# Row copies from HBM to HBM for 14 of 128 tiles in a rank scatter on Trainium2

## The chip, the cores and the metric

The kernel runs on one core of a Trainium2 chip. The metric is the device time of one execution in microseconds (us). The time before is the median of three runs.

## What is computed

Each of eight batches has 2048 rows of 2560 float32 values (10240 bytes a row) and one score for each row. A row is written to the place that its score has in the ascending order of its batch. No row value is changed, so apart from the ranks the whole work is moving 167.8 MB from one place in HBM to another.

```python
B, N, D = 8, 2048, 2560
order = np.argsort(scores, axis=1)
ranks = np.argsort(order, axis=1)
out = np.zeros_like(x)
out[b_idx, ranks, :] = x      # b_idx = np.arange(B)[:, None]
```

## The kernel before

A tile is 128 consecutive rows of one batch, 1.31 MB; there are 16 tiles in a batch and 128 in all. A tile is loaded from HBM into one of 16 SBUF buffers (`xb`, one row in each partition), and later scattered from there to HBM by an indirect DMA that takes a row number for each partition from `rank_i`.

**Ranks.** The scores come in by one small DMA. TensorE transposes them into columns (line 140), then for each batch copies each column across all partitions (`broadcast`, lines 156 to 169) so that every partition holds all 2048 scores of the batch in `s_all`. For a tile, VectorE counts how many scores of the batch are smaller than each of its 128 scores, and how many equal ones stand ahead of it (`count`, line 225, in two or three pieces), adds the pieces (lines 248 and 254) and casts the rank to an integer (line 265). VectorE goes through batches and tiles in order.

**The order by hand.** The whole body is one critical section in which every wait is written out: a `Line` object stands for an engine and counts its finished instructions on a semaphore. Three queues move the data:

- SP and ACT issue the loads in turn (`load`, lines 289 to 296; loop at lines 325 to 332): even tiles on SP, odd tiles on ACT. Load k waits until scatter k - 16 has landed, because it takes that scatter's buffer (`scatter_done`, line 298). ACT does nothing else.
- POOL issues the scatters in tile order (lines 355 to 363). Scatter k waits until load k has landed and until VectorE has written the rank of that tile.
- After the last load, SP waits for the last 16 scatters (lines 338 and 339).

**What is there and unused.** `DIRECT` (line 56) lists, for each batch, tiles that don't go through SBUF. In the kernel before it is empty, so `BULK` (line 61) has all 128 tiles and `ROWS` (line 62) none; `chunks` (line 323) is empty, and the loops at lines 329 and 333 do nothing. The code for such tiles is complete:

- `from_psum` (lines 179 to 199) and line 270: TensorE transposes the column of 128 ranks into one row in PSUM, and VectorE turns it into byte offsets in `rows_i`, on one partition. This is done one tile later, when the next tile's rank has been added up.
- `rows` (lines 304 to 320) takes one chunk, 16 rows of a tile: it waits for that tile's offsets, loads the 16 offsets into registers of SP or ACT, and issues 16 DMAs, each of which copies one row of 10240 bytes from `x` to `out` at the offset in a register.

```python
while n < len(chunks) * (k - NBUF + 6) // (NB - NBUF + 6 + 6):
    rows(*two[n % 2], *chunks[n])
    n += 1
load(two[k % 2][0], k)
```

This loop sets how the chunks stand among the loads: even chunks on SP, odd ones on ACT, in proportion to the number of loads issued.

Of the kernel before, what the change touches and what calls it, by code (L numbers as in the profile page):

```python
# [40 lines left out]
def kernel(  # L41
# [7 lines left out]
    B, N, D = x.shape  # L49
# [3 lines left out]
    T = N // P  # L53


    DIRECT = [()] * B

    SPLIT = ()
    LAST = 2
    ORDER = [list(range(T)) for b in range(B)]  # L60
    BULK = [(b, t) for b in range(B) for t in ORDER[b] if t not in DIRECT[b]]
    ROWS = [(b, t) for b in range(B) for t in DIRECT[b]]
    NB = len(BULK)
# [28 lines left out]
    with tc.tile_critical(no_gpsimd_drain=True):  # L92
# [86 lines left out]
        def from_psum():  # L179
            b, t, tick = pending  # L180
            dve.after(pe, tick)
            col = b * T + t
            if t in DIRECT[b]:
                t_rows[b, t] = dve.did(
# [16 lines left out]
        for b in range(B):  # L201
# [12 lines left out]
            for t in ORDER[b]:  # L214
# [43 lines left out]
                if pending is not None:  # L258
                    from_psum()
                    pending = None  # L260
                direct = t in DIRECT[b]
                if not direct:
# [131 lines left out]
```

## Time and profile before

| what | value |
|---|---|
| median of three runs (lowest, highest) | 798.27 us (798.03, 798.38) |
| profiled execution, its own time | 798.03 us |
| span of the profiled execution | 796.3 us |
| bytes moved by the DMA queues | 335.74 MB, mean 422 GB/s |
| VectorE busy | 422.3 us |
| TensorE busy | 29.3 us |
| POOL busy (issuing 128 scatters, 949 ns each) | 122.6 us |
| last load issued, last scatter issued | 738.9 us, 749.2 us |

Times within the execution count from the span's start. "Busy" counts the work of an engine; waiting and the issue of DMAs by SP and ACT are not in it. The profile cuts the span into 40 equal slices of 19.9 us, and gives for each slice the busy share of each engine in tenths (9 is 90% or more), the busy share of the 16 DMA engines, and the bytes that they moved. A byte that is loaded and then scattered is counted twice there, once for each transfer. A DMA's time "to landing" runs from its issue to its semaphore.

### The profile page before, as it was taken

To read this page: it belongs to the slowest core of one execution; us is meant where nothing else is said; L and a number is where in the kernel's file an instruction comes from. 1 tells how busy PE (TensorE), PEld (TensorE's weight loads), DVE (VectorE), ACT (ScalarE), POOL (GpSimd) and SP (SyncE) were. 2 spreads that over 40 slices of the span, in tenths; PEclk is the share of its full clock that TensorE was granted. 3 is DMA by queue.
4 is the path that set the end of the run, shared out by engine and by line. 5 is a ranking of instruction groups with operands and counts; after the bars stand their busy time and mean duration, and the time that the engine had idled before them with its cause. 6 is when DMAs were issued, how large, how long until landed. Compare 5 with 4: busy or idle time off the path is not lost.

```text
span 796.3 us, 1925 instructions
## 1 busy us (share of the span) xinstructions
PE 29.3 (4%) x144; PEld 26.4 (3%) x144; DVE 422.3 (53%) x1170; POOL 122.6 (15%) x136
## 2 busy tenths in 40 slices
PE   3001001010010010010000000000000000000000
PEld 3001001010010010010000000000000000000000
DVE  6999999999999999999999200000000000000000
POOL 1211121111111111111111111111111111111100
PEclk9555555555555555555555555555555555555555
DMA  9999999999999999999999999999999999999995
GB/s 360 423 429 427 428 429 429 428 429 427 429 427 429 428 430 429 430 428 428 428 428 428 430 430 430 428 429 429 428 428 430 430 430 429 428 429 428 428 430 219
DMA packets 36893, 335.74 MB, mean 422 GB/s; under 512 B 4104, under 2 KB 4104, under 8 KB 4104
## 3 DMA queue, kind: packets, MB, share of 16 engines
q0 software_dynamic: 18432, 167.78, 49.7%
q10 hardware_dynamic: 9216, 83.89, 24.9%
q1 hardware_dynamic: 9232, 83.96, 24.9%
q14 instruction: 12, 0.10, 0.0%
q8 instruction: 1, 0.02, 0.0%
HBM read 167.84 MB, written 167.77 MB: 421 GB/s over the span
## 4 chain that ended last, share of the span: by engine, by line
another core or an unknown queue 81%; DMA 7%; DVE 3%; ACTq 2%; PE 1%; issue 0%; POOL 0%; SPq 0%; POOLq 0%
DMA out_dram<-x,rank_i 6%; ACTq L294 2%; DVE trash L225 2%; DMA x<-in_x_dram 1%; PE ps_all L161 0%; DMA s_in<-in_scores_dram 0%; PE ps_col L140 0%; DVE rank L254 0%; DVE rank L248 0%; POOL out_dram L345 0%; DVE rank_i L265 0%; DVE s_all L206 0%; DVE s_col L148 0%; SPq L389 0%
## 5 line engine op out<-in xcount | busy, mean ns | idle before, releaser
L225 DVE TENSOR_SCALAR_CACHE_REDUCE trash<-s_all,s_col 128x256 bf16<-128x256 f32 (+15 forms) x248 | 315.1, 1307 | 0.3
L345 POOL DMA_INDIRECT out_dram<-x,rank_i x128 | 121.5, 949 | 626.7 <-DMA x<-in_x_dram 435.6
L225 DVE SCALAR_TENSOR_TENSOR trash<-s_all,s_col,mask 128x128 bf16<-128x128 f32 x128 | 44.5, 347 | 0.0
L161 PE MATMUL ps_all<-ident,s_col 128*128 128x128 f32 x128 | 27.4, 403 | 307.8 <-DVE s_all L206 307.4
L161 PEld LDWEIGHTS ps_all<-ident,s_col 128*128 128x128 f32 x128 | 24.6, 215 | 310.3 <-DVE s_all L206 309.8
L254 DVE TENSOR_TENSOR rank<-rank,acc 128x1 f32<-128x1 f32 x128 | 20.5, 160 | 4.4
L248 DVE TENSOR_TENSOR rank<-acc,acc 128x1 f32<-128x1 f32 x128 | 20.4, 159 | 4.4
L265 DVE CAST rank_i<-rank 128x1 int32<-128x1 f32 x128 | 19.7, 154 | 4.5
L206 DVE COPY s_all<-ps_all 128x512 f32<-128x512 f32 x32 | 20.2, 684 | 2.2 <-PE ps_all L161 1.6
L225 DVE DVE_READ_ACCUMULATOR trash<-s_all,s_col 128x1 f32 x248 | 20.5, 83 | 0.0
L225 DVE DVE_READ_ACCUMULATOR trash<-s_all,s_col,mask 128x1 f32 x128 | 10.5, 82 | 0.0
L148 DVE COPY s_col<-ps_col 128x128 f32<-128x128 f32 x1 | 0.3, 292 | 4.6 <-PE ps_col L140 4.6
L140 PE MATMUL ps_col<-ident,s_in 8*128 8x8 f32 x16 | 1.9, 250 | 4.0 <-DMA s_in<-in_scores_dram 4.0
L140 PEld LDWEIGHTS ps_col<-ident,s_in 8*128 8x128 f32 x16 | 1.8, 216 | 4.0 <-DMA s_in<-in_scores_dram 4.0
L135 DVE MEMSET acc<- 128x128 f32 x1 | 0.2, 165 | 1.1 <-SPq L92 1.1
L111 POOL TENSOR_SCALAR_AFFINE_SELECT ident<-ident 128x128 f32<-128x128 f32 x1 | 0.3, 283 | 0.1
L123 POOL TENSOR_SCALAR_AFFINE_SELECT mask<-mask 128x128 f32<-128x128 f32 x1 | 0.3, 283 | 0.0
L107 POOL MEMSET ident<- 128x128 f32 x1 | 0.2, 204 | 0.5 <-SPq L92 0.5
L108 POOL MEMSET mask<- 128x128 f32 x1 | 0.2, 202 | 0.0
L378 POOL MEMSET const-float32-0.0<- 128x1 f32 x1 | 0.1, 99 | 0.3 <-issue 0.3
L378 POOL MEMSET const-uint8-127<- 128x1 uint8 x1 | 0.1, 120 | 0.0
L378 POOL MEMSET const-bfloat16-1.0<- 128x1 bf16 x1 | 0.1, 114 | 0.0
(1 smaller groups left out, 0.1 us busy)
## 6 DMA issues: line engine op xcount, KB each, us to landing
x<-in_x_dram ACTq DMA_DIRECT2D x64, 1280.0 KB
x<-in_x_dram SPq DMA_DIRECT2D x64, 1280.0 KB, 10.3
out_dram<-x,rank_i POOLq DMA_INDIRECT x128, 87.4
s_in<-in_scores_dram SPq DMA_DIRECT2D x1, 64.0 KB
```

The source lines that it names most:

```text
L111: nc.gpsimd.affine_select(out=ident[:], in_=ident[:], pattern=[[-1, P]], compare_op=OP.not_equal, fill=1.0, base=0, channel_multiplier=1,)
L123: nc.gpsimd.affine_select(out=mask[:], in_=mask[:], pattern=[[-1, P]], compare_op=OP.is_ge, fill=0.0, base=-1, channel_multiplier=1,)
L140: nc.tensor.transpose(out=ps_col[:, B * c:B * (c + 1)], in_=s_in[:, P * c:P * (c + 1)], identity=ident[:B, :B],)
L161: nc.tensor.transpose(out=ps_all[:, P * c:P * (c + 1)], in_=s_col[:, c, b:b + 1].to_broadcast([P, P]), identity=ident[:],)
L206: nc.vector.tensor_copy(out=s_all[:, 512 * q:512 * (q + 1)], in_=ps_all[:, 512 * q:512 * (q + 1)],)
L225: how.pop("do")(out=trash[i][:, :P * (hi_t - lo_t)], in0=s_all[:, P * lo_t:P * hi_t], accum_out=acc[which][:, cols], **how,)
L248: nc.vector.tensor_tensor(out=rank[:, cols], in0=acc[0][:, cols], in1=acc[1][:, cols], op=OP.add)
L254: nc.vector.tensor_tensor(out=rank[:, cols], in0=rank[:, cols], in1=acc[2][:, cols], op=OP.add)
L265: nc.vector.tensor_copy(out=rank_i[:, cols], in_=rank[:, cols])
L294: line.eng.dma_start(out=xb[i][:], in_=x[b, P * t:P * (t + 1), :]).then_inc(s_load[i], 16)
L345: nc.gpsimd.indirect_dma_start(out=out_flat, out_offset=bass.IndirectOffsetOnAxis(ap=index[:hi - lo, col:col + 1], axis=0), in_=xb[k % NBU ...
L378: nc = _bacc.Bacc("TRN2", target_bir_lowering=False, num_devices=1)
```

## The change

Two tiles (numbers 4 and 5) in each of the first six batches and one (number 4) in each of the last two are put on the list `DIRECT`; the rest of the code stays.

```diff
@@ -53,7 +53,7 @@
     T = N // P
 
 
-    DIRECT = [()] * B
+    DIRECT = [(4, 5)] * 6 + [(4,)] * 2
 
     SPLIT = ()
     LAST = 2
```

By it, 14 tiles (1792 rows) leave the load and scatter path. `BULK` has 114 tiles, so SP and ACT issue 57 loads each and POOL issues 114 scatters. `chunks` has 112 entries, 56 on each of SP and ACT, each with 16 register loads and 16 row copies; six of them stand ahead of load 16, eight behind the last load. For the 14 tiles TensorE does one more transpose and VectorE does the offset instruction at line 185 in place of the cast at line 265. Before the end, SP and ACT wait for all of their row copies (line 337).

## The prediction

> **What bounds the kernel now.** I read the slices first.
>
> ```profile
> DVE  6999999999999999999999200000000000000000
> POOL 1211121111111111111111111111111111111100
> DMA  9999999999999999999999999999999999999995
> GB/s 360 423 429 427 428 429 429 428 429 427 429 427 429 428 430 429 430 428 428 428 428 428 430 430 430 428 429 429 428 428 430 430 430 429 428 429 428 428 430 219
> ```
>
> The DMA row is full from the first slice to the middle of the last, at 427 to 430 GB/s in almost all of them. VectorE stops after slice 23 and the rate doesn't change: the ranks don't bound it. So the 16 DMA engines do. Then the queues:
>
> ```profile
> q0 software_dynamic: 18432, 167.78, 49.7%
> q10 hardware_dynamic: 9216, 83.89, 24.9%
> q1 hardware_dynamic: 9232, 83.96, 24.9%
> ...
> HBM read 167.84 MB, written 167.77 MB: 421 GB/s over the span
> ```
>
> Scatters (q0) take half of the engines' time, the loads of ACT (q10) and SP (q1) a quarter each, 99.5% together. Each DMA has 144 packets: 128 rows and one semaphore packet on each of 16 engines. Last, the issues and the queue waits:
>
> ```profile
> x<-in_x_dram SPq DMA_DIRECT2D x64, 1280.0 KB, 10.3
> out_dram<-x,rank_i POOLq DMA_INDIRECT x128, 87.4
> ```
> ```profile
> SPq L294 <- DMA out_dram<-x,rank_i: 708.0, 56, 24.3
> ```
>
> A load lands 10.3 us after its issue, a scatter after 87.4 us: some 14 scatters are always queued, at one each 6.1 us. SP spends 708 us waiting for scatters to free a buffer. SP and ACT are nearly idle: 64 issues at a median of 328 and 334 ns (by line 294's view) are 21 us each. In the chain of waits, the steady pieces come 12.22 us apart (702.57, 714.79, 727.01), for two tiles, so one transfer of 1.3107 MB costs 12.22 / 4 = **3.055 us**.
>
> [...] No run shows it yet; I take it, so a row becomes 16 pieces of 640 bytes and 16 semaphore packets. [...] At the start, 17 issues of SP and ACT lie between 0.97 and 5.87 us, 0.29 us apiece over both queues, while a lone one takes 0.33: the trace agrees that two queues don't issue twice as fast.
>
> **The change, part by part.**
>
> *14 loads and 14 scatters go.* 28 x 3.055 = **85.5 us** of all 16 engines, all on the path, since nothing else bounds.
>
> *1792 row copies come.* Each byte passes an engine once, not twice. The trace shows no copy from HBM to HBM, so the price is bounded. Lower end, bytes alone at the steady rate: 18.35 MB / 429 GB/s = 42.8 us. [...] That is 35.5 ns x 1792 = **63.6 us**, which I take[...]. The net gain is 85.5 - 63.6 = **21.9 us** (ends: 42.7 faster, 34.5 slower). A row breaks even at 85.5 / 1792 = 47.7 ns per engine.
>
> *Issue on SP and ACT.* Each queue issues 56 chunks. A row's issue isn't in the trace; the nearest row is the load's, 0.33 us alone, 0.58 with both queues issuing (2 x 0.29). [...] 56 x 12.5 = 700, plus 49 loads x 0.33 = 16, plus the 30 us ahead of the first chunk: 746 us. It lies beside the transfers, under 776 us by only 30; cost nothing as long as a row takes less than (776 - 46) / 896 = **0.81 us** of its queue.
>
> *Queued behind the chunks.* A load behind a chunk starts up to 12.5 us late on its queue. POOL waits for it, but the 14 scatters already in the queue are 14 x 3 us of transfers even if no load runs, so the engines keep work. Nothing lost. At the start three chunks stand ahead of load 16 on SP (issued at 30.2 us before) and three on ACT. Their offsets exist once tile 5's rank is added, at about 30 us by the VectorE timeline; the loads then leave near 30 + 3 x 12.5 = 68 us. By then the engines can do 68 / 3.055 = 22 transfers; they have 16 loads and, at one rank per 3.2 us, about 14 scatters, plus 96 rows. Covered by 8 transfers, 24 us; without that cover the delay would show in full.
>
> *VectorE, TensorE, POOL.* The offset instruction replaces a cast of 154 ns, on 14 tiles; VectorE is done at about 445 us. Its wait for TensorE's transpose (403 ns for the nearest matmul row) comes after a whole tile's work of 3.2 us and is over by then. POOL loses 14 issues of 0.95 us while it is idle 626.7 us. Zero. Each is hidden by the DMA transfers.
>
> *The end.* Four chunks on each queue follow the last load: 4 x 12.5 = 50 us. Before, the last load left at 738.9, 57.4 us ahead of the end, so they fit by 7 us. Zero, with a few us at risk.
>
> **Sum.** The profiled execution took 798.03 us (span 796.3, 1.7 around it), 0.24 below the median. 798.03 - 21.9 = 776.1, so **776** on the median's scale (776.4).
>
> **Rivals.**
>
> *Slower: SP and ACT bind.* Mechanism: the row copy's issue with its register load, on the two queues, exceeds 0.81 us per row; then loads, which stand in line between the chunks, come late and the scatter queue runs dry. [...] the queues need 46 + 896 x 0.93 = **880 us**. For it: 0.78 at my middle price is near the limit. Against it: a row has 32 packets where a load has 144[...].
>
> *Slower: packets cost more than 47.7 ns.* At the upper end of 67 ns: 798.3 - 85.5 + 120 = **833 us**. [...]
>
> *No gain.* An HBM to HBM copy costs what its read and its write cost apart (2 x 42.8 = 85.6): **798 us**. For it: the page counts read and written bytes at 421 GB/s together. [...]
>
> *More gain.* [...] 798.3 - 85.5 = **713 us**. Against it: the trace counts busy DMA engines, 99.5%, and the copies need these too.
>
> **Numbers.** My forecast holds 755 to 797 (rows at 24 to 47 ns), chance 0.75; more gain 0.04; no gain 0.05; dear packets 0.04; issue binds 0.12. About 0.2% is what a measurement of this kernel can tell from no change. Faster 0.75 + 0.04 = 0.79, same 0.05, slower 0.16. From 753 to 800 lie the forecast and the no-gain case, 0.80.
>
> **What would show it.** Right: about 1792 x 16 small data packets, 317 MB moved, the DMA row at 9 throughout, SP and ACT still waiting for scatters (over 30 us in total), and a scatter's time to landing well above 10 us. The row copies' share of engine time, 63.6 / 776 = 8%, gives the price per row. Wrong: a scatter lands soon after its issue and the DMA row drops to 8 or below (issue binds), or that share is at 11% or more (dear packets), or a row comes as one packet on one engine, which would load that engine alone.

## The result, and the profile after

| | before | after |
|---|---|---|
| median (lowest, highest) | 798.33 us (798.03, 798.54) | 942.49 us (942.36, 943.91) |
| span of the profiled execution | 796.3 us | 940.7 us |
| ratio after to before | | 1.181, 95% interval 1.179 to 1.183 |

The change makes the kernel 18% slower. The forecast was 776 us, the range 753 to 800. In the slices of the kernel after, one view, two rows:

```profile
DMA  9999999999999999999988899999999999999761
GB/s 365 428 428 416 356 382 359 342 371 340 367 339 364 325 357 333 323 368 328 348 294 301 284 368 340 369 329 376 332 352 328 353 327 331 357 342 339 277 247 26
```

After four slices near the old rate the second row falls to between 284 and 382 GB/s and stays there until the end takes it lower still, while the first shows nines in most slices: busy engines and moved bytes have come apart. The queues of the kernel after (packets, MB, share of the 16 engines' span):

```profile
q0 software_dynamic: 16416, 149.43, 37.8%
q10 hardware_dynamic: 36880, 83.95, 29.9%
q1 hardware_dynamic: 36896, 84.01, 26.1%
```

Scatters had 49.7% and now have 37.8%; ACT and SP move the bytes that they moved before, in four times as many packets. The DMA issues of the kernel after (count, KB each, median us to landing where the view gives it):

```profile
x<-in_x_dram ACTq DMA_DIRECT2D x57, 1280.0 KB
x<-in_x_dram SPq DMA_DIRECT2D x57, 1280.0 KB
out_dram<-in_x_dram SPq DMA_DIRECT2D x896, 10.0 KB
out_dram<-in_x_dram ACTq DMA_DIRECT2D x896, 10.0 KB
out_dram<-x,rank_i POOLq DMA_INDIRECT x114, 14.7
```

The last line answers to the 87.4 us of before: a scatter lands 14.7 us after its issue, so the row of waiting scatters that fed the engines is gone. Who SP waits for, in the kernel after:

```profile
SPq L306 <- DVE trash L225: 28.6, 5, 25.7
SPq L92 <- DMA out_dram<-in_x_dram: 5.9, 1, 5.9
```

The line on top before, 708 us of waiting for scatters, has no successor. After its first ranks SP waits for nothing; it issues all the time. Its timeline in the middle of the kernel after (start, length, line and operation, count):

```profile
409.15 0.83 SPq L294 DMA_DIRECT2D x<-in_x_dram  x1
411.09 14.55 SPq L316 DMA_DIRECT2D out_dram<-in_x_dram  x16
425.69 0.57 SPq L294 DMA_DIRECT2D x<-in_x_dram  x1
427.38 14.62 SPq L316 DMA_DIRECT2D out_dram<-in_x_dram  x16
442.06 0.79 SPq L294 DMA_DIRECT2D x<-in_x_dram  x1
```

A load leaves every 16.4 us, with one chunk of 16 rows between two loads. ACT does the same, so the kernel advances two tiles per 16.4 us where it took 12.2 before. The end follows: the first row leaves at 31.6 us, the last at 931.4, 900 us for 56 chunks of 16.07 us.

**Where the time is, by packets.** A packet, as the trace records it with its length in time, is one piece that an engine moves, or one increment of a semaphore. Before, a 10240-byte packet took 385 ns on its engine and a semaphore packet 9. Sums over all packets, divided by 16 engines, within the span; idle time is 16 less the packets under way at each moment:

| | before | after | difference |
|---|---|---|---|
| scatters' packets | 394.5 us | 354.2 us | -40.3 |
| loads' packets | 395.7 us | 428.8 us | +33.1 (14 loads fewer: -43.3; slower packets: +76) |
| row copies with their semaphores | 0 | 96.6 us | +96.6 (at 32 + 9 ns: 73.5; slower packets: 23) |
| idle engine time | 11.7 us | 74.1 us | +62.4 |

These come to 152 us; moments with more than 16 packets under way take 8 back, and the span grew by 144.4. What the 14 tiles save, 83.6 us, is nearly used up by the rows at their own price, 73.5; the loss is idle time and packets that run slower.

### The profile page after: what moved, and what is told of

It reads as the page before. It is cut to its first block, busy times and chain, and to the rows that moved or that the text cites. A ratio compares the mean times of both kernels' runs of the same rounds, so it can differ in the third digit from the quotient of the medians.

```text
span 940.7 us, 5605 instructions
## 1 busy us (share of the span) xinstructions
PE 33.8 (4%) x158; PEld 27.1 (3%) x158; DVE 422.0 (45%) x1170; POOL 109.7 (12%) x122
## 3 DMA queue, kind: packets, MB, share of 16 engines
q0 software_dynamic: 16416, 149.43, 37.8%
## 4 chain that ended last, share of the span: by engine, by line
issue 50%; DVE 42%; POOL 4%; PE 1%; DMA 0%; POOLq 0%; SPq 0%
DVE trash L225 34%; POOL out_dram L345 4%; DVE rank L248 2%; DVE rank L254 2%; DVE s_all L206 2%; DVE rank_i L265 2%; DMA s_in<-in_scores_dram 0%; PE ps_all L161 0%; DVE rows_i L185 0%; PE ps_col L140 0%; POOLq L28 0%; DVE s_col L148 0%; SPq L389 0%; SPq L92 0%
## 5 line engine op out<-in xcount | busy, mean ns | idle before, releaser
L345 POOL DMA_INDIRECT out_dram<-x,rank_i x114 | 108.6, 952 | 802.0 <-DMA x<-in_x_dram 634.1
L265 DVE CAST rank_i<-rank 128x1 int32<-128x1 f32 x114 | 17.3, 152 | 3.7
L270 PE MATMUL ps_row<-ident,rank 128*1 128x128 f32 x14 | 5.2, 372 | 160.1 <-DVE rank L254 142.8
L185 DVE TENSOR_SCALAR rows_i<-ps_row 1x128 int32<-1x128 f32 x14 | 3.8, 272 | 0.0
## 6 DMA issues: line engine op xcount, KB each, us to landing
out_dram<-x,rank_i POOLq DMA_INDIRECT x114, 14.7
```

What stands on the lines that cost most here:

```text
L185: nc.vector.tensor_scalar(out=rows_i[ROWS.index((b, t))][:], in0=ps_row[:1, :P], scalar1=float(b * N), scalar2=float(ROW), op0=OP.add, op1 ...
L265: nc.vector.tensor_copy(out=rank_i[:, cols], in_=rank[:, cols])
L270: nc.tensor.transpose(out=ps_row[:1, :P], in_=rank[:, cols], identity=ident[:])
L345: nc.gpsimd.indirect_dma_start(out=out_flat, out_offset=bass.IndirectOffsetOnAxis(ap=index[:hi - lo, col:col + 1], axis=0), in_=xb[k % NBU ...
```

## The experiments

The theories, under the letters that the expectations use. **A**: SP and ACT bind, because issuing a row is dear in itself. **B**: the engines bind, because rows are dear to them. **C**: loads stand behind rows in one queue, and a row in a queue with others gets on slowly. **D**: A and C in one: a row's DMA takes its queue 0.65 us, longer while the queues are full, so that loads leave late. **D1** supposes why longer: the queues take turns at each engine, packet by packet, so a row waits behind packets of the other queues. **D2** stands for any cause of the longer time that doesn't depend on the length of those packets.

### Eight and four direct tiles: m8, m4

```diff
-    DIRECT = [(4, 5)] * 6 + [(4,)] * 2
+    DIRECT = [(4,)] * 8                  # m8
+    DIRECT = [(4,)] * 4 + [()] * 4       # m4
```

> One direct tile in each batch, 8 in all. Theory A (the issue on SP and ACT binds; the engines pay little for a row, 35.5 ns): each queue has 32 chunks of 15.7 us, 30 + 32 x 15.7 + 60 x 0.7 = 574 us, so issue no longer binds and the time is 798.3 - 8 x 6.11 + 1024 x 0.0355 = 786 us, faster than the kernel before. Theory B (the engines bind: in the changed kernel SP's and ACT's queues hold the engines 56.0% of 940.7 us, 114 loads of 3.10 us are 353 of it, the rest is 97 ns per row): 798.3 - 48.9 + 1024 x 0.097 = 849 us, slower.

> One direct tile in each of the first four batches. Theory A: issue is far from binding, 798.3 - 24.4 + 512 x 0.0355 = 792 us. Theory B: 798.3 - 24.4 + 512 x 0.097 = 824 us. A straight line through 0, 4 and 8 tiles would be for B, a bend between 8 and 14 for A.

Measured: 836.49 us with eight tiles (ratio 1.047, 1.046 to 1.049), 798.59 with four (1.0005, 0.9998 to 1.0013). No theory gave these: the curve through 0, 4, 8 and 14 tiles is 798, 799, 836, 942. A as a pure issue bound at a fixed price is wrong at eight, where 574 us of issue would fit easily. B as a fixed price per row is wrong at four. In the packet records of m4 each of a row's 640-byte packets takes 32 ns and its semaphore packet 9, so the engines' own price is 41 ns, not 97; 97 ns was a mean that held other things.

### Rows alone: rows_only

```diff
-        for k in range(NBUF):
-            load(two[k % 2][0], k)
...
-        for k, (b, t) in enumerate(BULK):
...
```

> The 114 loads and scatters are left out; ranks and the row copies of the 14 tiles stay. Theory A (a row's issue has a price of its own): 30 + 56 x 15.7 = 909 us with nothing beside it. Theory B (a row is slow to issue because the engines are full): the rows alone need 174 us of the engines, and the issue falls to the load's 0.33 us, 30 + 56 x (16 x 0.33 + 1.5) = 410 us.

Measured: 672.91 us. Line 316 of rows_only (shortest, median, longest in ns, first and last start):

```profile
L316 SPq DMA_DIRECT2D out_dram<-in_x_dram x896: 517/547/1317, 30.8 to 666.2; - x180
L316 ACTq DMA_DIRECT2D out_dram<-in_x_dram x896: 524/550/1618, 30.9 to 667.2; - x180
```

Both theories missed. With the engines nearly empty a row still takes 0.55 us to issue, 0.65 from one to the next, and with the register load of each chunk (one instruction of about 1.0 us for 16 registers) 896 rows take 636 us: 0.71 each. The register loads of rows_only:

```profile
L306 SPq TENSOR_LOAD <-rows_i x56: 968/972/1172, 29.6 to 655.5; - x56
L306 ACTq TENSOR_LOAD <-rows_i x56: 1005/1017/1203, 29.6 to 656.5; - x56
```

The price of a row's issue is real, more than a load's 0.33, but well under the 0.98 that A took from the full kernel.

### Rows to fixed places: static_rows

```diff
-            _, at = nc.values_load_multi_w_load_instructions(...)
...
-                    out=out_bytes[bass.ds(at[i], ROW)],
+                    out=side_bytes[r + i, :],
```

> As the changed kernel, but each row copy goes to a fixed place in a side buffer in HBM, so no offset is loaded to a register; the 14 tiles' rows are left out of the output. If the register and what hangs on it make the issue dear (A), a row falls to 0.33 us and the time to 776 us. If any DMA of one row is dear to issue, it stays near 940 less 56 x 1.5 for the register loads, 857 us. If the engines bind (B), 798.3 - 85.5 + 174 = 887 us.

Measured: 939.14 us (ratio 1.175, 1.173 to 1.177), as the change. The registers and their loads are not the cost. The rows' lines in the kernel after, then in static_rows:

```profile
L316 SPq DMA_DIRECT2D out_dram<-in_x_dram x896: 3/634/2349, 31.6 to 931.4; - x180
L316 ACTq DMA_DIRECT2D out_dram<-in_x_dram x896: 524/574/2622, 31.6 to 927.9; - x180
L310 SPq DMA_DIRECT2D side<-in_x_dram x896: 488/711/3342, 30.7 to 924.5; - x180
L310 ACTq DMA_DIRECT2D side<-in_x_dram x896: 496/674/3019, 30.7 to 923.6; - x180
```

When the register loads go, the median issue of a row rises to 674 ns on ACT and 711 on SP, and the last row starts hardly earlier. Something else sets the pace.

### One DMA for 16 rows: sixteen_rows, pieces

```diff
-            for i in range(G):
-                line.eng.dma_start(...)
+            line.eng.dma_start(
+                out=side[r:r + G, :],     # pieces: 640 bytes each, 768 apart
+                in_=x[b, P * t + G * q:P * t + G * (q + 1), :],
+            ).then_inc(s_rows[line], 16)
```

> The 14 tiles go from HBM to a side buffer in HBM, 16 rows in one DMA of 16 pieces of 10240 bytes, 112 DMAs in place of 1792; the 14 tiles' rows are left out of the output. If the engines charge a copy from HBM to HBM like any transfer of its bytes (24 ns per 640 bytes), the time is 798.3 - 85.5 + 43 = 756 us. If they charge read and write apart, 798 us. If the bytes of such a copy are the cost of the change (B: 97 ns per 640 bytes), 887 us.

> As the run before, 16 rows in one DMA, but in pieces of 640 bytes, to a side buffer that holds them 768 bytes apart: the row copies' pieces without a DMA and a semaphore for each row. If the size of the pieces is the cost, B's 97 ns per piece: 887 us. If it isn't, [...] 798.3 - 85.5 + 55 = 768 us.

Measured: 754.57 us with 10240-byte pieces (ratio 0.945, 0.943 to 0.947) and 763.06 with 640-byte pieces (0.956, 0.954 to 0.958), where 768 was the author's estimate. B is out. A copy from HBM to HBM costs an engine what one transfer of its bytes costs (packets of 385 ns, as for loads), and small pieces add 8.5 us. The waiting row of scatters is untouched in sixteen_rows:

```profile
out_dram<-x,rank_i POOLq DMA_INDIRECT x114, 93.2
```

So the same bytes on the same path gain 44 us when 112 DMAs carry them (35 in the small pieces), and lose 141 when 1792 do.

In pieces, though, the row of waiting scatters is gone as it is in the change, and a load takes 10 us to issue on SP:

```profile
L295 SPq DMA_DIRECT2D x<-in_x_dram x57: 358/9962/15988, 1.5 to 693.8; - x57
out_dram<-x,rank_i POOLq DMA_INDIRECT x114, 14.6
```

Yet its slices stay at 420 to 429 GB/s from the third to the last but one. Neither a scatter that lands soon nor an issue that is held up is a loss as such; it is one where the engines run short of work or their packets run slower, as in the change.

### Rows and loads in separate queues: m8_split, pool_loads

m8_split has eight tiles, all rows on ACT and all loads on SP; pool_loads has the change's 14 tiles, with the loads on POOL.

```diff
-            load(two[k % 2][0], k)
+            load(sp, k)                              # m8_split
-                rows(*two[n % 2], *chunks[n])
+                rows(*two[1], *chunks[n])            # m8_split
+            if k + AHEAD < NB:                       # pool_loads, AHEAD = 8
+                load(pl, k + AHEAD)
```

> Eight direct tiles, all row copies on ACT, all tile loads on SP. Theory C (tile loads stand behind row copies in one DMA queue, and rows go through a queue one after the other at 0.7 us or more, so buffers fill late and the scatters run out): with the loads in a queue of their own the 8 tiles cost only the engine time of 42 ns per row seen with four tiles, 798.3 - 48.9 + 1024 x 0.042 = 792 us; ACT needs 30 + 1024 x 0.714 = 761 us. Theory B (engine time rises with the number of rows, 72 ns with eight tiles): 798.3 - 48.9 + 74 = 823 us or, as with mixed queues, 836 us.

> The 14 tiles of the change; the 114 tile loads are issued by POOL, eight tiles ahead of the scatters, and SP and ACT issue row copies alone. Theory C: rows take 30 + 56 x 11.4 = 668 us as they do alone, loads never stand behind them, and the time is 798.3 - 85.5 + 1792 x 0.042 = 788 us. Theory A (a row takes 0.9 us of its queue in a full kernel): 30 + 896 x 0.98 = 908 us. Theory B: 887 us or more.

pool_loads took 799.73 us (ratio 1.0017, 1.001 to 1.0024): with the loads out of the rows' way, 143 of the 144 us are gone with the same 1792 row DMAs on the same two queues. That is C's direction, against A and B. But the rows got faster too:

```profile
L316 SPq DMA_DIRECT2D out_dram<-in_x_dram x896: 517/538/1030, 34.6 to 736.8; - x180
```

They take 0.78 us each, with the register loads (896 of them from 34.6 to 736.8 us), so pool_loads doesn't tell late loads from slow rows. m8_split does. It took 1093.11 us (1.369), far from C's 792, and two windows of it show why (length, then busy times, granted clock, DMA share, GB/s at the end of the line):

```profile
60.00:700.00 640.00, 24.36 (x103) 20.07 (x103) 370.47 (x1029) 96.52 (x101) 0.72 1.02 425
800.00:1080.00 280.00, 0.00 (x0) 0.00 (x0) 0.00 (x0) 0.00 (x0) 0.50 0.08 15
```

The tiles are moved at 425 GB/s, undisturbed, and are done by about 760 us; then rows are left and go on alone. So slow rows don't slow the tiles when no load stands behind them. In the trace, the stretch from 50 to 690 us has 479 rows, 1.34 us each (the long issues last 1.48 to 1.50 us); alone, one takes 0.71. The same instruction in the same queue is almost twice as slow beside two full queues.

### Two rows in one DMA, shorter chunks: pairs, static_g4

```diff
-            for i in range(G):                       # pairs: 896 DMAs of two rows
+            for i in range(0, G, 2):
-    G = 16                                           # static_g4: chunks of four rows
+    G = 4
```

> As the run with fixed row copies (side buffer, the 14 tiles' rows left out of the output), but two rows in one DMA, in the same pieces of 640 bytes: 896 row DMAs in place of 1792. Theory D (SP and ACT are taken up by the issue of 0.65 us per DMA, longer while their queues are full, so that loads come late): a chunk needs 8 x 0.65 = 5.2 us, 56 of them 290 us, the queues run ahead again, and the time is that of 16 rows in one DMA with 784 more semaphore packets per engine at 9 ns, 763 + 7 = 770 us. If turns at the engines alone are the cost (32 packets per chunk before, 24 here, 17 with 16 rows in one DMA): 763 + 176 x 7 / 15 = 845 us.

> As the run with fixed row copies, but the chunks have 4 rows in place of 16, four times as many and spread evenly between the loads; the same number of DMAs on each queue. Theory D: the queues are as much taken up as before, 939 us (925 to 950). If the length of a chunk ahead of a load is the cost (each load up to 16 rows late, in bursts): a quarter of the lateness, toward 835 us.

Measured: 808.98 us for pairs (ratio 1.013, 1.012 to 1.015), 928.12 for static_g4 (1.163, 1.161 to 1.165). Both write to a side buffer, as static_rows does. Chunks of four rows change little, so it isn't the length of one chunk ahead of a load but how long all of them hold the queue. Half the DMAs recover 130 of the 141 us between static_rows and before; the time lies between D's 770 and the 845 that turns alone gave, so neither working alone gives it.

### Other loads on POOL: m8_pool, pool_ahead12, m0_pool

```diff
+    DIRECT = [(4,)] * 8          # m8_pool
+    DIRECT = [()] * B            # m0_pool
+        AHEAD = 12               # pool_ahead12
```

> Eight direct tiles, loads on POOL, SP and ACT issue row copies alone. Theory D: 798.3 - 8 x 6.11 + 1024 x 0.041 = 791 us, and up to 10 more for the end, where with 14 tiles 23 us of engine time lay idle; in any case far under the 836 us of eight tiles with the loads on SP and ACT.

> The 14 tiles with loads on POOL, issued 12 tiles ahead of the scatters in place of 8. If the idle end of the run before is a matter of how far the loads run ahead, it goes and the time falls toward 786 us; if some of the 16 engines are simply behind the others, it stays at 800 us.

> No direct tile; the loads are issued by POOL eight tiles ahead. If loads on POOL cost nothing of their own: 798 us, and then rows beside them neither gain nor lose. If the late end of the runs with POOL's loads (18 GB/s in the last 20 us) comes from POOL's loads: about 815 us, and 14 tiles of rows gain about 15 us there.

All three have the loads on POOL, as pool_loads. Measured: 800.34 us (ratio 1.0025, 1.0016 to 1.0034), 804.80 (1.0075, 1.0062 to 1.0089) and 808.84 (1.013, 1.011 to 1.014). Loads further ahead made it worse: of the two cases that pool_ahead12 was to tell apart, 786 us is out, and even 800 was passed. m0_pool has no rows and is 10 us slower than before, so moving the loads to POOL costs that by itself; beside this price, 14 tiles of rows gain 9 us. The slices of m0_pool show where:

```profile
GB/s 345 407 430 427 428 429 428 428 426 427 429 429 427 427 429 430 427 427 429 430 429 428 427 430 430 428 428 429 431 428 428 429 430 429 428 428 430 430 427 48
```

The rate is the old one, but the last slice has 48 GB/s where it had 219, and the DMA row shows a 1 there: most of the engines' time is idle. Why the rest are late was not tried.

### Half-size packets beside the rows: m8_split_half, m14_half

```diff
-            line.eng.dma_start(
-                out=xb[i][:], in_=x[b, P * t:P * (t + 1), :]
-            ).then_inc(s_load[i], 16)
+            for h in (0, D // 2):
+                line.eng.dma_start(
+                    out=xb[i][:, h:h + D // 2],
+                    in_=x[b, P * t:P * (t + 1), h:h + D // 2],
+                ).then_inc(s_load[i], 16)
```

The scatters are halved in the same way, with twice the rank as the index of a half row. m8_split_half is otherwise m8_split, and m14_half is otherwise the change.

> Eight direct tiles, rows on ACT and loads on SP as in the run at 1093 us, but each tile is loaded and scattered as two halves of 1280 columns, so the packets beside the rows have 5120 bytes. D1: with two full queues beside it a row waits 2 x (0.193 + 0.193) = 0.77 us in place of 2 x 0.77 = 1.54; during the tiles a row takes 0.8 to 0.9 us in place of 1.34, about 850 rows are done by 750 us, and the end comes near 880 us. D2: rows stay at 1.34 us and the time near 1093 us.

> The change as it is (rows and loads mixed on SP and ACT), with the tiles loaded and scattered in halves of 5120-byte packets. D1: the blocked part of the issue, about 4.5 us of the 16.4 us that a chunk and its load take on a queue, falls by half: 56 x 2.3 = 126 us less, 815 us, or 850 if the second load issue per tile and the added packets take some of it back. D2: 940 us, or a little more for the added issues.

Measured: m8_split_half 801.90 us (ratio 1.005, 1.003 to 1.006) against 1093 with whole packets. The row's line in it:

```profile
L321 ACTq DMA_DIRECT2D out_dram<-in_x_dram x1024: 524/550/847, 33.6 to 772.6; - x171
```

The median is the 550 ns of rows alone, the longest 847, and a row takes 0.72 us all the way, with both other queues as full as before (417 GB/s). Nothing on ACT was changed, SP issues twice as many loads, and the engines have more packets to handle, not fewer (101935 against 67373); only the packets that a row waits behind are half as long. That speaks for D1 and against D2: the wait follows the length of those packets. The numbers of m8_split fit a turn for each 10240-byte packet. A row has 32 packets for 16 engines; with a data and a semaphore packet on each, two turns behind two packets of 0.385 us are 2 x 2 x 0.385 = 1.54 us (an estimate), and the long issues measured 1.48 to 1.50. The starts of m8_split's rows agree: of 473 steps between 60 and 700 us, 173 are 1.55 to 1.60 us long and 97 are 1.15 to 1.20, some four and three packets; 74 are 0.60 to 0.70, a row that isn't held up. In this reading not every turn meets a packet of both queues, so the mean of 1.34 us is below the full two turns. By the same share half packets would let a row through every 0.70 us (an estimate: two turns of 2 x 2 x 0.196 us and 0.04 for the row's own packets, times 1.34 / 1.58), about what the issue takes anyway, which may be why the run went further than D1's 0.8 to 0.9. The turns themselves are on no view; they are the author's reading of these lengths.

m14_half took 877.04 us (1.097, 1.096 to 1.099), 65 us less than the change, D1's direction at about half its size: in mixed queues the length of the packets beside a row is a part of the loss.

### Four tiles, rows in a queue of their own: m4_split

```diff
-    DIRECT = [(4, 5)] * 6 + [(4,)] * 2
+    DIRECT = [(4,)] * 4 + [()] * 4
...
+            load(sp, k)
...
+                rows(*two[1], *chunks[n])
```

> Four direct tiles, all their rows on ACT, all loads on SP. At 1.34 us per row beside two full queues ACT needs 30 + 512 x 1.34 = 716 us, so it doesn't bind, and the loads never stand behind a row. The engines' prices give 798.3 - 4 x 6.11 + 512 x 0.041 = 795 us, a gain of 0.4%, against 798.6 us with mixed queues.

Measured: **792.64 us**, ratio 0.9926 (0.9912 to 0.9940), 2 us below what was expected, and the one version with the whole computation that beats both kernels. In it:

```profile
L316 ACTq DMA_DIRECT2D out_dram<-in_x_dram x512: 524/1154/1836, 33.1 to 706.0; - x171
```

The rows are still slow (median 1154 ns), but ACT is done at 706 us, as 30 + 512 x 1.34 = 716 foretold, and no load waits for them. Their time from issue to landing here, then in rows_only:

```profile
DMA to landing us min/median/max: 5.4/47.5/51.9
DMA to landing us min/median/max: 1.9/2.1/3.5
```

At 1.34 us a row, 47.5 us are some 35 rows in the queue (an estimate), and the longest time, 51.9, is not much more. With an issue of 1154 ns where a row alone has 550, the author reads this as a full queue and an issue that waits for room. Against m4, the same four tiles in mixed queues, m4_split is 6 us faster. The slices put that at the end and not into the steady part: both move 421 to 430 GB/s from the third slice on, but the last slice has 100 GB/s in m4 and 213 here.

## Why the prediction was wrong

**The 85.5 us of the transfers that go: right in size.** 28 transfers at 3.055 (by the packets 40.3 + 43.3 us went); sixteen_rows, where only this and the bytes of the copies count, took 754.57 us where the lower end of the working gave 755.6.

**The rows' price on the engines: right in its packets, a little small.** A row does come as 16 pieces and 16 semaphore packets: beside 57 loads of 144 packets, q10 has 28672 packets left for 896 rows, 32 each. 35.5 ns, 63.6 us, was the step, and 67 ns its upper end; both were the author's estimates, which no trace of before showed. Beside full engines (m4, pieces) the packets measure 32 + 9 = 41 ns, 73.5 us. In the changed kernel, where packets run slower, a row comes to 54 ns, over the 47.7 at which it breaks even; how much of that comes from the next step is open. The pieces without a semaphore for each row were worth 763 us. The upper end and the rival "no gain" at 798 us are refuted, and so is "more gain".

**The issue on SP and ACT: the step that failed.** It said 12.5 us per chunk, 0.78 per row, a limit of 0.81, hence no cost. Of the 0.78, the issue of 0.58 came from the trace; the rest, for the register, was the author's estimate. Measured: 16.07 us per chunk with its load, some 0.96 us per row without the load, over the limit. The sum had the wrong parts: registers cost about 0.06 us each (one load instruction of 1.0 us for 16, in rows_only), much less than the estimate, and a row's issue 0.65, not 0.58. Together 0.71 alone (rows_only), even under the step's price; had that held, the queues would have been free at about 680 us (30 + 896 x 0.71 + 16). What was left out, a term put at nothing, is that a row takes its queue longer in company: 1.34 us beside two full queues of 10240-byte packets (m8_split), 0.72 beside two of half-size packets (m8_split_half). An issue that is held up while its queue is full, and a queue that empties at the pace of D1's turns, fit both, as the author reads them. That was not a price on any row of the profile of before; m8_split and m8_split_half show it for rows in a queue of their own, and m14_half shows a part of it in the changed kernel, 65 of 144 us.

**"Queued behind the chunks: nothing lost": failed with it.** The cover named there, 14 waiting scatters, holds only while loads leave ahead of their need (a scatter lands 14.7 us after its issue now, 87.4 before). Each load is now issued behind a chunk on a queue that is never free, so the stock of scatters is used up once and not refilled: the first four slices are near the old rate, the rest isn't. That loads behind the rows turn slow rows into a slow kernel shows in m8_split, whose tiles go on at 425 GB/s beside rows of 1.34 us, and in pool_loads, where 143 us come back.

**The rival "SP and ACT bind" was the right one.** It gave 880 us at 0.93 per row and was given a chance of 0.12. The direction came as written, and of its signs the scatter that lands soon, with SP no longer waiting; the DMA row's drop to 8 or below came in only six of 40 slices, since slower packets keep that row full. Its price was near by luck: what it charged for a register was an estimate that no trace of before showed, far above the 0.06 us that rows_only measured, and it knew nothing of rows that get slower beside full queues. What was held against it, that a row has fewer packets than a load and so a shorter issue, was wrong: 32 packets took 0.55 us to issue (rows_only), a load's 144 took 0.33 (before).

**The start, VectorE and TensorE: right.** The rows begin at 31.6 us, VectorE is busy for 422.0 us as before, and the first slices are full, though the first load behind SP's three chunks leaves at 80 us and not at 68. The end, foretold as covered by 7 us, has engines waiting: the last load leaves at 874.6 us, 66 us ahead of the end, with rates of 277, 247 and 26 GB/s in the last three slices.

**What stays open.** In the changed kernel 20% of the load packets on ACT's queue and 13% on SP's took over 500 ns, though their bytes are the same; in m8_split and pool_loads, with no rows in the loads' queue, it is at most 0.5%, as before. This is most of the 76 us of slower packets in the table. Rows in the loads' queue are not enough for it: in m4 and in pieces the share is at most 0.6%, in m8 it is 2 to 4%. So it comes with many row DMAs, like the loss, and whether it is a cause of it or a consequence isn't shown. Nor is the split of the loss between turns and plain issue time exact in mixed queues: m14_half recovers 65 us of 144, pairs 130 of 141.

## What to carry to other kernels

When a transfer is cut into many DMAs, price the queue that issues them in the company that it will have: here 0.71 us for a row alone became 1.34 beside two full queues of 10240-byte packets, and half-size packets brought 0.72 back. Keep prefetching loads off a queue that issues many small DMAs: the same 1792 copies cost 144 us in the loads' queues and 1 us with the loads on POOL. A stock of waiting scatters is cover only as long as someone refills it in time, so read "who waits for a free buffer" and the bytes per slice before and after: when the loader no longer waits and the slices fall, it has become the bound. The first sign alone isn't enough: in pieces the loads hardly wait for buffers, and the slices stay full.

## What the runs showed of the hardware

- One row of 10240 bytes from HBM to HBM, in 16 pieces: 0.55 us of issue on SP or ACT, 0.65 from one to the next (rows_only); with a fixed address the shortest issue is 0.03 us shorter, 488 ns for 517 on SP and 496 for 524 on ACT (static_rows). It lands 2.1 us after its issue when no load or scatter moves (rows_only).
- Beside full engines, an HBM to HBM packet of 10240 bytes holds an engine 385 ns, like a load's or a scatter's; one of 640 bytes 32 ns; a semaphore 9 ns (sixteen_rows, pieces, m4).
- Beside two full queues of 10240-byte packets ACT's queue takes a row every 1.34 us in the mean, most often 1.55 to 1.60 (m8_split), and every 0.72 us beside two of 5120-byte packets (m8_split_half). In m4_split some 35 rows stand in it, an estimate from 47.5 us to landing at 1.34 us a row.
- One instruction loads 16 registers from SBUF in 0.97 us on SP and 1.02 on ACT (rows_only).
- HBM reads and writes together came to 446 GB/s over the span in sixteen_rows, an estimate: its engines moved 317.40 MB, 421 GB/s, and the 18.35 MB of the copies among them were both read and written.
